# Down projection by products: when staged pieces are loaded and split, where S2 is computed, who evicts the first sums, and when the residual is added

## The chip, the cores and the metric

The kernel runs on one core of a Trainium2 chip. The metric is the device time of one execution in microseconds (us). The engines named below are TensorE (PE in the profile, with its weight loads as PEld), VectorE (DVE), ScalarE (ACT), GpSimd (POOL), and SyncE (SP), whose queue issues nearly all DMA transfers of this kernel.

## The reference, cut to what matters

The program is a two-layer decoder trunk over 1024 tokens of width 1024, in float32. Each layer has a mixer and a gated feed-forward part; the change concerns the last matrix product of the feed-forward part, in both layers.

```python
D_MODEL = 1024; SEQ = 1024; DEPTH = 2; D_FF = 2816

def conv_glu_ffn(x, w_up, conv_w, conv_b, w_down):
    h = causal_depthwise_conv(x @ w_up, conv_w, conv_b)
    gate, val = jnp.split(h, 2, axis=-1)
    return (jax.nn.silu(gate) * val) @ w_down      # (1024 x 2816) @ (2816 x 1024)

for layer in range(DEPTH):
    h = h + mixer(rmsnorm(h, ...))                 # even_mixer or odd_mixer
    h = h + conv_glu_ffn(rmsnorm(h, ffn_norm[layer]), ffn_up[layer], ffn_conv_w[layer],
                         ffn_conv_b[layer], ffn_down[layer])
return rmsnorm(h, final_norm)
```

## The kernel before, in words

**Precision.** Every float32 operand is *split*: ACT casts it to float32r (the high part, `h`), and DVE subtracts that from the source (the low part, `l`; "the low" in what follows). The function `split` does both. A product of two operands is three matmuls, hi·hi, hi·lo and lo·hi, each of a 128x128 weight block with a 128x512 block of tokens.

**The stage.** The 2816 hidden values are 22 blocks f of 128. Blocks 0 to 15 go through the down projection in two groups g of eight (`EIGHTS`), blocks 16 to 21 (`PLAIN`) directly and afterwards. Within a group the weights and the hidden values are cut into 2 x 2 blocks and multiplied with seven block products in place of eight (Strassen's scheme in Winograd's form). The hidden side's sums for that (`hids`, in DRAM) are made in the up projection that runs before. The weight side's sums are made in the stage: S1 = x21 + x22, S2 = S1 - x11, x11 - x21, and later S4 = x12 - S2.

**Quads and products.** Four output blocks form a quad: `Quad(g, oc, form)` with oc 0 or 4. A quad of form A makes the products "11", "2", "3" and "4" (with x11, S2, x11 - x21 and x22), a quad of form B makes "1", "21" and "22" (with S1, x12 and S4). Their order is, for each g: A oc 0, A oc 4, B oc 0, B oc 4. These are 28 products per layer (`steps_`), each of two half-products e of 12 matmuls, so 56 places t in one stage. The matmuls' tiles carry the quad's name: dq000A is layer 0, g 0, oc 0, form A; dq114B is layer 1, g 1, oc 4, form B. In instruction lists the product and e follow (dq000A111: product 11, e 1).

**Preparation of weights.** Two steps ahead of each product, `prep` runs the quad's step: load, sums and split of its weights (`x11`, `s2`, `s3`, `x22` for A, `s1`, `x12`, `s4` for B). S1 and S2 are stored to DRAM (`sums`) by the A quad and loaded again by the B quad. Whole weights come into two buffers (tag wst), half ones into four (`t2`), split weights wh and wl into three.

**Pieces.** The hidden side of a product comes in two *pieces* of 512 KB. `bring` loads one into a buffer br (a ring of four, tag t4, which the up projection also uses) and splits it at once into AH/AL (products 11, 2, 3, 4) or TH/TL (products 1, 21, 22). `stage` does the same with a plain block (hr), and `residual_in` loads 512 KB of the residual (hd) and adds it to hT, the sum that all products end in. The list `beside` holds such calls by group and form; one is taken behind each half-product as long as the list lasts.

**Evictions.** Four PSUM banks of 128x512 are used. After every half-product the bank's running sum goes to hT: by ACT as a copy where nothing stands in hT yet (group 0, oc 0, form A; L929), otherwise by DVE as an addition (L931). The residual lies in DRAM (hdr); half of it is loaded straight into hT for oc 4 at the start of the stage (L1058), the other half comes through `residual_in` in the second group.

**Order.** The code lists the work; a scheduler then orders each engine's instructions by its own estimates of times, and `tc.issue_after(x)` keeps what is issued under it behind x. Each engine, and each queue, then runs in order. The last block of the up projection (f = 21) has edits too: its Tail does the convolution's taps (L690), gate and store (`hid` and cv, L707) of the block before, while the first quad's weights and pieces come in.

## Time and profile before

| What | Value |
| --- | --- |
| Median of 3 runs | 2156.36 us (2156.1 to 2157.13) |
| Profiled execution | 2156.32 us, its span 2154.6 us |
| TensorE, busy | 2102.5 us, 98% of the span |
| DVE, busy | 1599.4 us, 74% |
| ACT, busy | 1062.9 us, 49% |
| Granted TensorE clock, mean | 0.996 |
| First to last product matmul, layer 0 | 781.91 to 947.19 us |
| First to last product matmul, layer 1 | 1907.00 to 2073.48 us |
| Loads of pieces (L808) | 56 of 512 KB, 5.5 us from issue to landing (median) |

Times in rows of the trace count from the start of the span. A row of a timeline reads: start, duration, engine (SPq is SyncE's queue), line, operation, what it writes and from what, shape, count, and in brackets the idle time of the engine just before with what ended it. Rows of a window read: stretch, its length, then the busy time and number of instructions of PE, PEld, DVE, ACT and POOL, the granted clock (1.00 is full speed), the share of the DMA engines that was busy, and GB/s. Rows of waits read: engine, its tile and line, what it waited for, total us, times, the longest.

### The profile page before, as it was taken

What the parts mean: (1) busy time and instruction counts of PE and PEld (TensorE: products, weight loads), DVE (VectorE), ACT (ScalarE), POOL (GpSimd) and SP (SyncE); (2) the same over time, 40 slices, a digit from 0 to 9 for tenths busy, and PEclk for the clock granted to TensorE, in tenths of its full rate; (3) what the DMA queues carried; (4) which work ended last, traced back from release to release, by engine and by line L of the source; (5) the groups of instructions that cost most, each with busy time, mean ns of one, the idle gap of its engine ahead of it and who ended that gap; (6) DMA issues with size and microseconds to landing.
All of it is one profiled execution on the core that took longest, in us unless ns stands there. A gap on an engine that the chain in (4) does not pass through costs nothing. (4 is left out here: it accounts for less than half of the span.)

```text
span 2154.6 us, 25867 instructions
## 1 busy us (share of the span) xinstructions
PE 2102.5 (98%) x9673; PEld 1720.3 (80%) x9673; DVE 1599.4 (74%) x2306; ACT 1062.9 (49%) x1485; POOL 74.7 (3%) x121
## 2 busy tenths in 40 slices
PE   8999999999999999999999999899999999999998
PEld 7888888788888877788778888788788888877787
DVE  6655647998888778855566666868998888778854
ACT  5333544655445554333556575744655554455323
POOL 0000001000000000000111111000000000000000
PEclk9999999999999999999999999999999999999999
DMA  4211342333232268641221211542333332268612
GB/s 145 59 49 44 108 147 92 103 103 118 94 117 94 77 208 301 229 126 64 74 65 47 83 50 55 166 148 88 98 123 98 98 117 93 98 229 281 222 49 79
DMA packets 265382, 249.98 MB, mean 116 GB/s; under 512 B 10384, under 2 KB 214992, under 8 KB 265256
## 3 DMA queue, kind: packets, MB, share of 16 engines
q1 hardware_dynamic: 264920, 247.83, 36.1%
q8 instruction: 76, 1.25, 0.2%
q0 software_dynamic: 192, 0.30, 0.1%
q14 instruction: 50, 0.41, 0.1%
q10 hardware_dynamic: 144, 0.20, 0.0%
HBM read 181.93 MB, written 64.26 MB: 114 GB/s over the span
## 5 line engine op out<-in xcount | busy, mean ns | idle before, releaser
L121 ACT CAST wh<-wst 128x1024 fp32r<-128x1024 f32 (+1 forms) x87 | 86.3, 992 | 224.6 <-PE op L368 45.1
L121 DVE TENSOR_TENSOR wl<-wst,wh 128x1024 fp32r<-128x1024 f32 (+1 forms) x87 | 100.1, 1151 | 98.4 <-ACT wh L121 98.2
L668 PE MATMUL X<-TH,wh 128*128 128x512 f32 x384 | 150.0, 391 | 1.8 <-ACT u L1012 1.4
L668 PE MATMUL X<-TH,wl 128*128 128x512 f32 x384 | 149.7, 390 | 0.7 <-DVE wl L362 0.7
L668 PE MATMUL X<-TL,wh 128*128 128x512 f32 x384 | 149.5, 389 | 0.0
L361 ACT CAST wh<-wst 128x1024 fp32r<-128x1024 f32 x96 | 100.2, 1050 | 74.2 <-PE YZ L668 49.6
L362 DVE TENSOR_TENSOR wl<-wst,wh 128x1024 fp32r<-128x1024 f32 x96 | 116.6, 1220 | 12.1 <-ACT wh L361 12.1
L690 DVE SCALAR_TENSOR_TENSOR cg<-g,par_c,cg 128x1023 f32<-128x1023 f32 x88 | 112.8, 1282 | 6.9 <-ACT cg L684 5.8
L690 DVE SCALAR_TENSOR_TENSOR cv<-v,par_c,cv 128x1023 f32<-128x1023 f32 (+1 forms) x88 | 112.5, 1278 | 0.1
L668 PE MATMUL YZ<-AH,wh 128*128 128x512 f32 x240 | 93.5, 389 | 0.0
L668 PE MATMUL YZ<-AL,wh 128*128 128x512 f32 x240 | 93.4, 389 | 0.0
L668 PE MATMUL YZ<-AH,wl 128*128 128x512 f32 x240 | 93.4, 389 | 0.0
L1012 ACT COPY u<-X 128x512 f32<-128x512 f32 x40 | 23.5, 587 | 138.0 <-PE X L668 138.0
L668 PEld LDWEIGHTS X<-TH,wh 128*128 128x128 f32 x384 | 72.1, 188 | 18.6 <-ACT u L1012 2.6
L668 PEld LDWEIGHTS X<-TH,wl 128*128 128x128 f32 x384 | 72.1, 188 | 16.6 <-DVE wl L362 1.6
L668 PEld LDWEIGHTS X<-TL,wh 128*128 128x128 f32 x384 | 72.1, 188 | 14.9
L1032 DVE TENSOR_TENSOR v<-p,u 128x512 f32<-128x512 f32 x40 | 27.7, 692 | 68.8 <-ACT u L1022 68.8
L368 PE MATMUL op<-AH,wh 128*128 128x512 f32 x192 | 76.3, 397 | 0.6 <-ACT hT_o L543 0.6
L368 PE MATMUL op<-AH,wl 128*128 128x512 f32 x192 | 74.9, 390 | 0.0
L368 PE MATMUL op<-AL,wh 128*128 128x512 f32 x192 | 74.8, 390 | 0.0
L684 ACT ACTIVATE cg<-g,par_c 128x1024 f32<-128x1024 f32 x44 | 54.8, 1246 | 28.8 <-DVE g L1034 24.2
L1557 ACT ACTIVATE P<-P,sm 128x128 f32<-128x128 f32 (+3 forms) x64 | 49.7, 777 | 29.9 <-DVE sm L1554 29.6
(815 smaller groups left out, 6305.2 us busy)
## 6 DMA issues: line engine op xcount, KB each, us to landing
wst<-in_ffn_up_dram SPq DMA_DIRECT2D x88, 512.0 KB, 3.8
br<-hids SPq DMA_DIRECT2D x56, 512.0 KB, 5.5
wst<-in_mix_w_in_dram SPq DMA_DIRECT2D x40, 512.0 KB, 3.7
wst<-in_mix_w_out_dram SPq DMA_DIRECT2D x32, 512.0 KB, 4.2
hids<-cv SPq DMA_DIRECT2D x32, 512.0 KB, 3.0
hdr<-hT_o SPq DMA_DIRECT2D x32, 256.0 KB, 2.0
hids<-t SPq DMA_DIRECT2D x32, 256.0 KB, 2.4
hid<-cv SPq DMA_DIRECT2D x12, 512.0 KB
```

The lines of the kernel that those rows point to most:

```text
L121: did = self.nc.scalar.copy(wh[:, :k, :m], w[:, :k, :m]), self.eng.tensor_tensor(wl[:, :k, :m], w[:, :k, :m], wh[:, :k, :m].bitcast(F32), ...
L361: return (act.copy(h, src), (eng or dve).tensor_tensor(l, src, h.bitcast(F32), op=ALU.subtract))
L362: (eng or dve).tensor_tensor(l, src, h.bitcast(F32), op=ALU.subtract))
L368: last_mm = pe.matmul(ps, a[:, k], b[:, k, s], start=(k == 0 and i == 0), stop=(k == DC - 1 and i == 2))
L668: last = pe.matmul(ps, a[:, k0 + k], b[:, k], start=(first and k == 0 and i == 0), stop=(k == 3 and i == 2), skip_group_check=True)
L684: act.activation(self.cg, self.g, AF.Identity, scale=taps[2](f), bias=bias(f))
L690: dve.scalar_tensor_tensor(dst[:, dl:], src[:, :T - dl], taps[j](c), dst[:, dl:], op0=ALU.mult, op1=ALU.add)
L1012: act.copy(u2, X)
L1032: dve.tensor_tensor(v[:, HALF[1]], p5, u3, op=ALU.add)
L1557: act.activation(Pt[:, :n], Pt[:, :n], AF.Exp, bias=low, scale=-1.0, accum_out=sm[:, 6:7])
```

## The change

The separate loads and splits: `bring`, `stage` and `residual_in` now issue the load at once and return a function that does the split (or the addition). A table by place t says where each split stands (`AT_FIRST` to `AT_PLAIN`); its load is issued `AHEAD` = 3 half-products earlier. A split is held behind the previous half-product's eviction and the last cast of weights. The first pieces come in the last block of the up projection.

S2 is written into the buffer of x11, split as one operand of 1024 columns, and stored by one transfer of 512 KB; x11 - x21 is therefore made in step `s2`, ahead of it. `sums` has another layout in DRAM. The first quad's x22 is loaded whole into the buffer that cv of block 20 leaves. Each later quad's first two weight loads are issued at two steps, no longer both at one.

All quads of form A in group 0 are evicted by ACT as copies. All eight parts of the residual are loaded and added at places in the second group. The store of the last hidden block (cv021 to `hid`) moves behind the first half-product.

```diff
@@ -41,2 +41,10 @@
+
+AHEAD = 3
+AT_FIRST = (2, 4)
+AT_B0 = (5, 7, 8, 10, 12, 14)
+AT_A1 = (15, 16, 18, 19, 21, 22, 24, 25)
+AT_B1 = (28, 30, 32, 34, 36, 38)
+AT_RES = (29, 33, 37, 41, 45, 47, 49, 51)
+AT_PLAIN = (43, 44, 46, 48, 50, 52)
 OPS = {"11": 0, "2": 1, "4": 2, "3": 3, "21": 4, "22": 5, "1": 6}
@@ -597,3 +605,3 @@
     hids = [[dram.tile([P, 7, 4, H], F32, name=f"hids{i}{g}") for g in EIGHTS] for i in range(2)]
-    sums = {(i, g, q): [dram.tile([P, 2, 4, P], F32, name=f"sum{i}{g}{q}{j}") for j in range(2)]
+    sums = {(i, g, q): [dram.tile([P, DC, P], F32, name=f"sum{i}{g}{q}{j}") for j in range(2)]
             for i in range(2) for g in EIGHTS for q in (0, 4)}
@@ -705,3 +713,5 @@
                 f, to, k = self.f, hids[ly][self.f // 8 % 2], self.f % 8 // 2
-                if f >= PLAIN[ly][0][0]:
+                if f == NF - 1:
+                    return
+                elif f >= PLAIN[ly][0][0]:
                     nc.sync.dma_start(hid[ly][:, f], self.cv)
...
@@ -794,3 +805,3 @@
             nc.sync.dma_start(r, hid[ly][:, f])
-            split(*slots[slot], r)
+            return lambda: split(*slots[slot], r)
...
@@ -845,3 +856,3 @@
                                                  name=f"{n}{self.name}")
-                    nc.sync.dma_start(t if n == "s1" else two(t), src)
+                    return nc.sync.dma_start(t if n == "s1" else two(t), src)
@@ -857,9 +868,15 @@
                     else:
-                        wst("x21", self.block(0, self.oc + 2, 2))
-                        small("x22", lambda e: self.block(1, self.oc + 2 + e, 1))
+                        last["sp"] = wst("x21", self.block(0, self.oc + 2, 2))
+                        if self.g == 0 and self.oc == 0:
+                            t = w2[1].tile([P, T], F32, tag="cv0", name=f"x22{self.name}")
+                            t = t.rearrange("p (k m) -> p k m", k=DC)
+                            nc.sync.dma_start(two(t), self.block(1, self.oc + 2, 2))
+                            self.raw["x22"] = [one(t, e) for e in range(2)]
+                        else:
+                            small("x22", lambda e: self.block(1, self.oc + 2 + e, 1))
                 elif i == 0:
-                    wst("s1", self.sum[0].rearrange("p e k m -> p (e k) m"))
+                    wst("s1", self.sum[0])
                 else:
                     wst("x12", self.block(1, self.oc, 2))
-                    small("s2", lambda e: self.sum[1][:, e])
+                    small("s2", lambda e: one(self.sum[1], e))
@@ -869,2 +886,5 @@
+            def whole(self, n, src):
+                last["cast"], last["low"] = split(*self.pair(n), src)
+
             def split2(self, n, src):
...
@@ -880,17 +900,16 @@
                 for e in range(2):
-                    dve.tensor_tensor(s[e], one(self.raw["x21"], e), self.raw["x22"][e],
-                                      op=ALU.add)
-                    nc.sync.dma_start(self.sum[0][:, e], s[e])
+                    last["sum"] = dve.tensor_tensor(s[e], one(self.raw["x21"], e),
+                                                    self.raw["x22"][e], op=ALU.add)
+                    nc.sync.dma_start(self.sum[0][:, 4 * e:4 * e + 4], s[e])
             def s2(self):
-                s = self.raw.pop("s")
+                t, a, s = self.raw["x21"], self.raw.pop("x11"), self.raw.pop("s")
+                dve.tensor_tensor(t, a, t, op=ALU.subtract)
                 for e in range(2):
-                    dve.tensor_tensor(s[e], s[e], one(self.raw["x11"], e), op=ALU.subtract)
-                    nc.sync.dma_start(self.sum[1][:, e], s[e])
-                self.split2("2", s)
+                    dve.tensor_tensor(one(a, e), s[e], one(a, e), op=ALU.subtract)
+                nc.sync.dma_start(self.sum[1], a)
+                self.whole("2", a)
             def s3(self):
-                t, a = self.raw.pop("x21"), self.raw.pop("x11")
-                dve.tensor_tensor(t, a, t, op=ALU.subtract)
-                split(*self.pair("3"), t)
+                self.whole("3", self.raw.pop("x21"))
...
@@ -927,6 +946,6 @@
                 at = st["hT"][:, self.oc + 2 * row + e, s]
-                if self.form == "A" and self.g == 0 and self.oc == 0:
-                    act.copy(at, ps)
+                if self.form == "A" and self.g == 0:
+                    did = act.copy(at, ps)
                 else:
-                    dve.tensor_tensor(at, ps, at, op=ALU.add)
+                    did = dve.tensor_tensor(at, ps, at, op=ALU.add)
                 if n in ("4", "21", "22"):
...
@@ -946,3 +966,3 @@
                 if q.form == "A":
-                    loads = {2: (0, 1)}.get(i, ())
+                    loads = {1: (0,), 2: (1,)}.get(i, ())
                 else:
@@ -993,2 +1013,3 @@
                 quads[0].load(0)
+                came = [b() for b in first_[:2]]
             w, nxt = ws.pop(f), f + 1 if f + 1 < NF else None
@@ -1011,3 +1032,8 @@
             u2 = t2(f"u2{ly}{f}")
-            act.copy(u2, X)
+            u2_ = act.copy(u2, X)
+            if not nxt:
+                with tc.issue_after(u2_.ins):
+                    for do in came:
+                        do()
+                came = [b() for b in first_[2:4]]
             prev.conv_v(0)
@@ -1027,5 +1053,2 @@
                 quads[0].load(1)
-                with tc.issue_after(u3_.ins):
-                    for b in first_[:2]:
-                        b()
             prev.sums()
@@ -1044,7 +1067,10 @@
             prev.ident()
-        for b in first_[2:4]:
-            b()
+        with tc.issue_after(u3_.ins), tc.issue_after(last["sum"].ins):
+            for do in came:
+                do()
         prep(1)
-        for b in first_[4:6]:
-            b()
+        came = [b() for b in first_[4:6]]
+        with tc.issue_after(last["cast"].ins), tc.issue_after(last["low"].ins):
+            for do in came:
+                do()
         prev.rest()
@@ -1056,4 +1082,2 @@
         hT = st["hT"]
-        for c in range(4, DC):
-            nc.sync.dma_start(hT[:, c], hdr[:, c])
@@ -1077,18 +1101,35 @@
             nc.sync.dma_start(r, hdr[:, c])
-            dve.tensor_tensor(hT[:, c], hT[:, c], r, op=ALU.add)
+            return lambda: (None, dve.tensor_tensor(hT[:, c], hT[:, c], r, op=ALU.add))
+
-        beside = {(0, "A"): first_[6:] + brings(0, ("1", "21", "22")),
-                  (0, "B"): brings(1, ("11", "2", "3", "4")),
-                  (1, "A"): [x for c, b in enumerate(brings(1, ("1", "21", "22")))
-                             for x in [b] + ([lambda c=c: residual_in(c)] if c < 4 else [])],
-                  (1, "B"): [lambda i=i: stage(PLAIN[ly][0][0] + i, i) for i in range(6)]}
+        pieces = {}
+        for at, ps in ((AT_FIRST, first_[6:]), (AT_B0, brings(0, ("1", "21", "22"))),
+                       (AT_A1, brings(1, ("11", "2", "3", "4"))),
+                       (AT_B1, brings(1, ("1", "21", "22"))),
+                       (AT_RES, [lambda c=c: residual_in(c) for c in range(DC)]),
+                       (AT_PLAIN, [lambda i=i: stage(PLAIN[ly][0][0] + i, i) for i in range(6)])):
+            for t, p_ in zip(at, ps):
+                pieces[t] = p_
+        came, prev_did = {}, None
         for n, (q, i) in enumerate(steps_):
-            todo = beside[q.g, q.form]
             for e in range(2):
-                q.prod(q.prods[i], e)
+                t = 2 * n + e
+                for t_ in range(t + 1 if t else 0, t + 1 + AHEAD):
+                    if t_ in pieces:
+                        came[t_] = pieces.pop(t_)()
+                did = q.prod(q.prods[i], e)
                 if e == 0 and n + 2 < len(steps_):
                     prep(n + 2)
-                if todo:
-                    todo.pop(0)()
+                if t == 0:
+                    with tc.issue_after(last["sp"].ins):
+                        nc.sync.dma_start(hid[ly][:, NF - 1], prev.cv)
+                    prev = None
+                if t in came:
+                    with ExitStack() as behind:
+                        behind.enter_context(tc.issue_after(last["cast"].ins))
+                        if prev_did is not None:
+                            behind.enter_context(tc.issue_after(prev_did.ins))
+                        came.pop(t)()
+                prev_did = did
             if n == len(steps_) - 2:
```

The first place is ACT's queue around the first quad of layer 0. AH and TH are the high parts of pieces br, wh those of weights; 0040 reads layer 0, group 0, product 4, piece 0; a bank keeps the name of product 11 for all four products; L929 and, after the change, L948 copy sums to hT. Before:

```order
L361 CAST wh68_5826<-x11004A_5743 128x1024
L361 CAST AH_83<-br0040_5751 128x2x512
L361 CAST AH_83<-br0041_5769 128x2x512
L929 COPY hT0_f0_5719<-dq000A110_5724 128x512
L929 COPY hT0_f0_5719<-dq000A111_5755 128x512
L361 CAST TH0_2559<-br0010_5792 128x1024
L929 COPY hT0_f0_5719<-dq000A110_5724 128x512
L929 COPY hT0_f0_5719<-dq000A111_5755 128x512
L361 CAST TH0_2559<-br0011_5809 128x1024
```

After:

```order
L948 COPY hT0_f0_5716<-dq000A110_5719 128x512
L369 CAST wh65_5686<-x11000A_5539 128x1024
L369 CAST AH_83<-br0030_5692 128x2x512
L369 CAST AH_83<-br0031_5694 128x2x512
L706 ACTIVATE cg021_5674<-cg021_5674 128x1024
L369 CAST wh66_5733<-x21000A_5633 128x1024
L948 COPY hT0_f0_5716<-dq000A111_5746 128x512
L948 COPY hT0_f0_5716<-dq000A110_5719 128x512
L369 CAST wh67_5775<-x22000A_5635 128x4x128 x2
L369 CAST AH_83<-br0040_5717 128x2x512
```

Before, the copies of the oc 0 quad come in pairs between the casts of pieces for products 4 and 1. After, the copy of half-product 0 of product 11 (dq000A110) stands first; two piece casts, the activation of the last up-projection block and a weight cast stand between it and the copy of half-product 1 (dq000A111).

The second place is SP's queue in the same stretch. Before:

```order
L808 DMA br0040_5751<-hids00_251 128x1024
L808 DMA br0041_5769<-hids00_251 128x1024
L707 DMA hid0_249<-cv021_5673 128x1024
L846 DMA x21004A_5745<-in_ffn_down_dram 128x4x256
L808 DMA br0010_5792<-hids00_251 128x1024
L1058 DMA hT1_f0_5715<-hdr_85 128x1024 x4
L808 DMA br0011_5809<-hids00_251 128x1024
L883 DMA sum0040_257<-s0004A_5830 128x512
```

After:

```order
L819 DMA br0031_5694<-hids00_251 128x1024
L910 DMA sum0001_256<-x11000A_5539 128x1024
L819 DMA br0040_5717<-hids00_251 128x1024
L857 DMA x11004A_5690<-in_ffn_down_dram 128x4x256
L819 DMA br0041_5744<-hids00_251 128x1024
L819 DMA br0010_5760<-hids00_251 128x1024
L857 DMA x21004A_5737<-in_ffn_down_dram 128x4x256
L819 DMA br0011_5796<-hids00_251 128x1024
L1126 DMA hid0_249<-cv021_5675 128x1024
L819 DMA br00210_5823<-hids00_251 128x1024
```

The residual loads into hT (L1058) are gone from between br0010 and br0011, S2 goes out in one store from x11's buffer (sum0001 from x11000A), and the store of cv021 stands behind br0011.

The third place is DVE's queue at the start of the second group's first quad (dq010A), where DVE evicts. TL is the low of a piece, wl that of a weight, hd a part of the residual. Before:

```order
L362 TENSOR_TENSOR wl80_6306<-x21010A_6188,wh80_6305 128x1024
L931 TENSOR_TENSOR hT0_f0_5719<-dq010A110_6290,hT0_f0_5719 128x512
L1078 TENSOR_TENSOR hT0_f0_5719<-hT0_f0_5719,hd00_6335 128x1024
L362 TENSOR_TENSOR TL0_2560<-br01211_6443,TH0_2559 128x1024
L931 TENSOR_TENSOR hT0_f0_5719<-dq010A111_6321,hT0_f0_5719 128x512
L362 TENSOR_TENSOR wl81_6352<-x220010A_6190,wh81_6351 128x4x128
L362 TENSOR_TENSOR wl81_6352<-x221010A_6191,wh81_6351 128x4x128
L881 TENSOR_TENSOR s0014A_6394<-x21014A_6311,x220014A_6313 128x512
L931 TENSOR_TENSOR hT0_f0_5719<-dq010A110_6290,hT0_f0_5719 128x512
L881 TENSOR_TENSOR s1014A_6395<-x21014A_6311,x221014A_6314 128x512
```

After:

```order
L370 TENSOR_TENSOR wl79_6264<-x11010A_6098,wh79_6263 128x1024
L950 TENSOR_TENSOR hT1_f0_5712<-dq004B11_6186,hT1_f0_5712 128x512
L370 TENSOR_TENSOR wl80_6299<-x21010A_6178,wh80_6298 128x1024
L370 TENSOR_TENSOR TL0_2560<-br0110_6226,TH0_2559 128x1024
L950 TENSOR_TENSOR hT0_f0_5716<-dq010A110_6284,hT0_f0_5716 128x512
L1102 TENSOR_TENSOR hT0_f0_5716<-hT0_f0_5716,hd00_6244 128x1024
L950 TENSOR_TENSOR hT0_f0_5716<-dq010A111_6312,hT0_f0_5716 128x512
L370 TENSOR_TENSOR wl81_6343<-x220010A_6180,wh81_6342 128x4x128
L370 TENSOR_TENSOR wl81_6343<-x221010A_6181,wh81_6342 128x4x128
L901 TENSOR_TENSOR s0014A_6382<-x21014A_6302,x220014A_6304 128x512
L370 TENSOR_TENSOR TL0_2560<-br0111_6269,TH0_2559 128x1024
L950 TENSOR_TENSOR hT0_f0_5716<-dq010A110_6284,hT0_f0_5716 128x512
```

Before, up to two weight lows, sums and a piece's low stand between the evictions of dq010A. After, S2's low and x11 - x21's low (wl79, wl80) and one piece (br0110) stand ahead of its first eviction, and the residual's addition comes between the first and the second.

11 lines of the change are left out of this document (6 added, 5 removed).

## The prediction

> **What bounds the kernel now.** I read the busy table first, then TensorE's waits, and then windows over the two stages that the change edits. TensorE is the bound: whatever is won or lost has to appear as TensorE waiting less or more.
>
> ```profile
> span 2154.6 us, 25867 instructions
> PE 2102.5 (98%) x9673; PEld 1720.3 (80%) x9673; DVE 1599.4 (74%) x2306; ACT 1062.9 (49%) x1485; POOL 74.7 (3%) x121
> ```
>
> The products of the down projection stand on L922 (tiles dq...). The windows of that line alone (columns: stretch, its length, PE busy with its number of matmuls, PEld busy, granted clock, DMA share, GB/s) are both stages, one undisturbed quad, and the two A quads of the second group in each layer:
>
> ```profile
> 781.91:947.19 165.28, 156.56 (x672) 126.09 (x671) 0.99 0.70 235
> 1907.00:2073.48 166.48, 158.04 (x672) 127.19 (x671) 0.98 0.68 228
> 851.87:868.19 16.32, 16.32 (x74) 13.51 (x72) 1.00 0.79 270
> 868.19:914.55 46.36, 44.57 (x194) 35.72 (x192) 1.00 0.67 222
> 1994.43:2040.84 46.41, 44.61 (x194) 35.72 (x192) 1.00 0.69 227
> ```
>
> The quad at 851.87 is 72 matmuls (the window touches two more) without idle time: 16.32 / 72 = 0.2267 us from start to start. A half-product (12) therefore takes 2.72 us, an A quad (96) 21.76, and a stage's 672 matmuls 152.3. The stages take 165.28 and 166.48, so **12.96 + 14.16 = 27.1 us** are lost in them. That is the ceiling of this change. Two A quads need 43.52; the second group takes 46.36 and 46.41, so 2.84 + 2.89 = 5.7 of the loss lie there, and 21.4 in the first group. Who TensorE waited for, in layer 0:
>
> ```profile
> PE dq004A L922 <- ACT wh L361: 3.6, 2, 3.2
> PE dq000A L922 <- DVE wl L362: 1.7, 2, 0.9
> PE dq010A L922 <- DVE hT_f L931: 1.4, 2, 1.2
> PE dq000A L922 <- ACT hT_f L929: 0.9, 1, 0.9
> ```
>
> Neither ACT nor DVE is short of time: they stand behind pieces that have not landed. In the same stretch ACT was idle 14.7 and 22.4 us for pieces (br), each a 512 KB load:
>
> ```profile
> L361 ACT CAST AH<-br 128x1024 fp32r<-128x1024 f32 x14 | 14.6, 1052 | 14.8 <-DMA br<-hids 14.7
> L361 ACT CAST TH<-br 128x1024 fp32r<-128x1024 f32 x12 | 12.6, 1050 | 24.5 <-DMA br<-hids 22.4 <-PE dq004B L922 2.1
> br<-hids SPq DMA_DIRECT2D x56, 512.0 KB, 5.5
> ```
>
> The largest wait, step by step: SP issues four residual loads and then a piece. The piece lands 9.2 us later, ACT's cast of it is released at 814.02, DVE's half of the split follows, and only behind that stand DVE's sum for S2, ACT's cast of it, and the matmul.
>
> ```profile
> 803.01 1.74 SPq L1058 DMA_DIRECT2D hT_f<-hdr  x4
> 804.85 1.29 SPq L808 DMA_DIRECT2D br<-hids  x1
> 814.02 1.05 ACT L361 CAST TH<-br 128x1024 fp32r<-128x1024 f32 x1 [3.52 <-DMA br<-hids]
> 815.10 1.22 DVE L362 TENSOR_TENSOR TL<-br,TH 128x1024 fp32r<-128x1024 f32 x1
> 816.25 0.69 DVE L888 TENSOR_TENSOR s0004A<-s0004A,x11004A 128x512 f32<-128x512 f32 x1
> 816.97 0.62 ACT L361 CAST wh<-s0004A 128x512 fp32r<-128x512 f32 x1 [1.89 <-DVE s0004A L888]
> 817.64 0.80 PE L922 MATMUL dq004A<-AH,wh 128*128 128x512 f32 x1 [3.22 <-ACT wh L361]
> ```
>
> **The change, part by part.** *Late residual and copies by ACT.* The 2 MB of residual loads at 803.01 leave the stretch; eight 512 KB loads now lie in the second group. Eight evictions of dq004A go from DVE to ACT, and four more residual adds come to DVE, per layer:
>
> ```profile
> L929 ACT COPY hT_f<-dq000A x8: 574/587/590, 787.2 to 809.9; 128x512 f32<-128x512 f32 x8
> L931 DVE TENSOR_TENSOR hT_f<-dq004A,hT_f x8: 684/688/692, 812.2 to 839.3; 128x512 f32<-128x512 f32 x8
> L1078 DVE TENSOR_TENSOR hT_f<-hT_f,hd x8: 1216/1222/1227, 871.8 to 2019.4; 128x1024 f32<-128x1024 f32 x8
> ```
>
> DVE: -8 x 0.688 + 4 x 1.222 = -0.6 us; ACT: +8 x 0.587 = +4.7. Both are free while TensorE is fed; the cover is the 43.5 us of the two A quads.
>
> *S2 in A11's place.* Per A quad two casts (0.62) and two lows (about 0.68) become one of each over 1024 columns (1.05 and 1.22), and x21 = x11 - x21 is only moved ahead: about -0.3 us. Two stores become one; S2's later loads become runs of 512 bytes, as those of x22 already are. I take nothing: these loads are used three products later.
>
> *The first A quad, walked.* I keep the clock of the profiled execution, where TensorE starts this quad at 781.9 in both versions, and take starts from these rows; a pair of lows takes 2.36 us, hence 1.15 from one to the next, and 0.6 for a half-width one.
>
> ```profile
> 770.43 0.32 SPq L707 DMA_DIRECT2D hid<-cv  x1
> 776.67 0.59 ACT L1022 COPY u<-X 128x512 f32<-128x512 f32 x1 [2.13 <-PE X L668]
> 778.23 2.36 DVE L362 TENSOR_TENSOR AL<-br,AH 128x1024 fp32r<-128x1024 f32 x2 [0.26 <-ACT AH L361]
> wst<-in_ffn_down_dram SPq DMA_DIRECT2D x3, 512.0 KB, 3.5
> hids<-cv SPq DMA_DIRECT2D x32, 512.0 KB, 3.0
> ```
>
> Now x22 is loaded whole into the buffer of cv, so SP must wait for that store: 770.4 + 3.0 = 773.4, landed at 776.9. Behind it in SP's queue stands one piece, which needs a low of 774.1 anyway. DVE, in its new order: x21 + x22 (776.9), v behind u3 (777.3), the other half (777.9), the low of br0020 (778.5), g (779.7), the low of br0021 (780.3), x21 (781.4), a tap (782.5), S2's halves (783.7 and 784.3, done 785.0), a tap (784.9). ACT casts S2 from 785.4 to 786.4, DVE lowers it from 786.5 to 787.7. TensorE's products 11 end at 787.35 and its third matmul of product 2 needs that low at 787.8: **no stall, against 0.80 and 0.89 us before**. Next ACT casts br0030, br0031, runs the silu and casts x21 before it copies the second bank of product 11; at 0.95 us each that copy ends near 790.7. TensorE wants it at 790.07: **0.65 us, and 0.1 of slow restart**. Product 4 needs the low of br0041 at 800.5; my walk has it at 800.35, so I charge another 0.5 for this and for S2's low together, with 0 and 1.5 as bounds. The second A quad (from about 804.5) finds x11, x21 and S2 ready five products ahead. First group: 2 x 1.25 = 2.5 left of 21.4.
>
> *The second group.* There DVE evicts, and one late piece blocks it:
>
> ```profile
> 874.60 1.05 ACT L361 CAST TH<-br 128x1024 fp32r<-128x1024 f32 x1 [5.34 <-DMA br<-hids]
> 875.69 1.22 DVE L362 TENSOR_TENSOR TL<-br,TH 128x1024 fp32r<-128x1024 f32 x1 [2.63 <-ACT TH L361]
> 876.83 0.68 DVE L931 TENSOR_TENSOR hT_f<-dq010A,hT_f 128x512 f32<-128x512 f32 x1
> 877.66 0.47 PE L922 MATMUL dq010A<-AH,wh 128*128 128x512 f32 x1 [1.16 <-DVE hT_f L931]
> 868.19:891.95 23.76, 22.38 (x97) 17.68 (x96) 20.39 (x26) 7.35 (x9) 0.00 (x0) 1.00 0.71 229
> ```
>
> The ring of four buffers lets a piece be issued four places before its split, 10.9 us, where 5.5 are needed, so these waits go. But DVE (20.39 busy in the last row) stays nearly full in 21.76; I leave 0.5 per layer (bounds 0 and 2.84). Left over in all: 2.5 + 1.0 = 3.5, so the change saves 27.1 - 3.5 = **23.6 us**. The profiled execution took 2156.32, 1.7 over its span and 0.04 under the median: 2132.7, said as **2133**.
>
> *One rule against the rows.* After the long wait the clock is halved, and in layer 1 too, where only 1.58 and 0.29 us of waiting precede:
>
> ```profile
> 817.30:820.70 3.40, 3.06 (x7) 2.44 (x8) 3.06 (x5) 3.40 (x5) 0.00 (x0) 0.51 0.95 269
> 1923.20:1926.60 3.40, 3.32 (x7) 2.28 (x8) 3.40 (x5) 1.36 (x3) 0.00 (x0) 0.51 0.86 334
> 1922.26 0.50 PE L922 MATMUL dq100A<-AH,wh 128*128 128x512 f32 x1 [1.58 <-ACT hT_f L929]
> ```
>
> A halved stretch gives 1.00 - 0.51 of 3.4, or 1.7 us, away. By these rows even two short waits close together could keep one per layer: 2136. The Trainium skill (TensorE: Matmul & The Clock Gate, Part 1) has the clock fall only after a whole idle window of about 3.4 us; by it the waits left over would never do this, and the sum stays. The row of 1923.20 disagrees with it.
>
> **The rivals.** (1) *The new wait bites.* x22's load waits for a store, and DVE's sum waits for x22 ahead of v, g and two pieces in its queue. For it: that queue is in order. Against: the DMA engines are idle then. If x22 lands 9.2 us after its issue, like the piece at 804.85, instead of 3.5, the chain moves by 5.7 us, TensorE waits 5.2 longer and runs 1.7 at half speed: 2 x 6.9 = 13.8 back, 2147.
>
> (2) *The first quad stays short of DMA.* Sixteen transfers of 0.52 MB stand between 778 and 805 in the new queue, 311 GB/s, and the stages' first groups ran at about that rate already. For it: a share of 0.95 at 269 GB/s above. Against: the residual's 2 MB are gone. If the first quads keep their waits, which are half of the first group's 21.4, and only the rest goes: 27.1 - 10.7 - 3.5 = 12.9 saved, 2143.
>
> (3) *Slower: the fixed places.* Each split is tied behind the eviction before it, and so stands ahead of the next one. From the last place of the first group's A quads on, where DVE evicts, there are 28 such places per layer. A weight's low, a piece's low and an eviction are 1.22 + 1.22 + 0.69 = 3.13 us against 2.72, or 0.41 over; with a sum (0.69) 1.1 over. If nothing carries to the lighter places and half of them have the sum, that is 56 places in both layers at 0.75 on average, 42 us: 2156 - 24 + 42 = 2174. It decides from 23.6 / 56 = 0.42 us per place. Against it: an eviction has a whole half-product of slack, since two banks alternate, and 20.39 us of DVE work fit 21.76.
>
> **How the numbers follow.** Forecast 0.62, own range 2129.5 to 2139 (nothing left over; the upper bounds 3.0 + 5.7 plus a clock loss per layer, less what cannot all come at once). Rival 1 0.16, rival 2 0.12, rival 3 0.07, and 0.03 for gains and losses that cancel. A measurement of this kernel tells about 0.2% (4.3 us) from no change: faster 0.62 + 0.16 + 0.12 = 0.90, same 0.03, slower 0.07. The range goes from 2129.5, nearly the ceiling of 27.1, to rival 1's 2147.
>
> **What would show it.** Right: both stages near 154 us; no wait of dq004A for ACT's cast; waits of dq000A for ACT's copy under 1 us; ACT's idle time for pieces down; no halved clock inside the stages. Wrong: x21 + x22 starting after 778 with DVE idle before it; dq010A waiting longer for evictions; a product waiting for a piece; the up projection's last block losing time, since its queues take the first pieces earlier. If TensorE runs through and the time still does not fall, the loss was never these waits.

## The result, and the profile after

The changed kernel takes **2138.32 us** (median of 4 runs, 2136.61 to 2143.3) where the kernel before takes 2156.23 beside it; the ratio is 0.9924, with a 95% interval of 0.9904 to 0.9944. It is 17.9 us faster. The forecast was 2133 (range 2129.5 to 2147): sign and range hold, the gain is three quarters of the 23.6 us that were forecast.

The first lines of the page after:

```profile
span 2136.6 us, 25861 instructions
PE 2097.7 (98%) x9673; PEld 1721.0 (81%) x9673; DVE 1599.6 (75%) x2290; ACT 1068.9 (50%) x1493; POOL 74.7 (3%) x121
```

The two windows over the product line (now L941), columns as in the prediction:

```profile
780.05:936.82 156.77, 153.77 (x672) 125.56 (x671) 1.00 0.72 237
1897.77:2055.31 157.54, 153.59 (x672) 125.59 (x671) 1.00 0.71 233
```

The stages took 165.28 and 166.48 us and take 156.77 and 157.54: 8.51 + 8.94 = 17.45 us of the 18.0 by which the span fell. Ahead of the first stage 1.86 us are gained, of which 1.3 are already there at 260 us, in code that did not change; between the stages 1.14 us are lost, and 0.17 behind them. TensorE's waits in the up projection ahead of the first stage are the same as before, within 0.1 us each. Against 152.34 us for 672 matmuls the stages now lose **4.43 + 5.20 = 9.6 us, where 27.1 were lost and 3.5 were forecast**. No clock below 1.00 is left in either.

The waits of TensorE in the two stages, in the form shown before:

```profile
PE dq014A L941 <- DVE hT_f L950: 1.1, 1, 1.1
PE dq000A L941 <- ACT hT_f L948: 0.8, 1, 0.8
PE dq000A L941 <- DVE wl L370: 0.5, 1, 0.5
PE dq000A L941 <- DVE AL L370: 0.4, 1, 0.4
...
PE dq114A L941 <- DVE hT_f L950: 1.4, 1, 1.4
PE dq100A L941 <- DVE AL L370: 1.1, 1, 1.1
PE dq100A L941 <- ACT hT_f L948: 0.9, 1, 0.9
PE dq100A L941 <- DVE wl L370: 0.5, 1, 0.5
```

dq004A's wait of 3.2 us for S2's cast is gone, and so is its twin in layer 1, which read before:

```profile
PE dq104A L922 <- ACT wh L361: 3.5, 2, 3.2
```

ACT's waits for pieces are gone too. In layer 0's stage it stood idle for 14.7 and 22.4 us for them; now the same rows (busy us and mean ns, then the idle time ahead) read:

```profile
L369 ACT CAST AH<-br 128x1024 fp32r<-128x1024 f32 x12 | 12.4, 1050 | 0.2 <-DMA br<-hids 0.2
L369 ACT CAST TH<-br 128x1024 fp32r<-128x1024 f32 x12 | 12.6, 1051 | 0.0
```

Four waits of TensorE are left per layer, the same four. A wait's row shows less than what it costs: counted from start to start of matmuls, with the late start and the slower first matmul after it, the four (S2's low, the copy, the low of br0041, the eviction in the second group) cost 1.21, 1.04, 0.69 and 1.36 us in layer 0 and 0.88, 1.22, 1.32 and 1.66 in layer 1. All other quads run at 21.76 and 16.32 us, without loss.

**S2's low.** SP issues x22 behind the store it waited for; DVE stands idle for it; then its queue runs without a gap to S2's low, and TensorE waits for that; 0.4 of the 1.21 us are already lost to S2's cast, just ahead of the low. From the timeline of layer 0:

```profile
771.84 0.38 SPq L873 DMA_DIRECT2D x22000A<-in_ffn_down_dram  x1
776.23 0.69 DVE L901 TENSOR_TENSOR s0000A<-x21000A,x22000A 128x512 f32<-128x512 f32 x1 [2.94 <-DMA x22000A<-in_ffn_down_dram]
785.78 1.23 DVE L370 TENSOR_TENSOR wl<-x11000A,wh 128x1024 fp32r<-128x1024 f32 x1
787.05 0.50 PE L941 MATMUL dq000A<-AH,wl 128*128 128x512 f32 x1 [0.52 <-DVE wl L370]
```

**The copy and br0041.** The copy of product 11's second bank stands behind a silu and a weight cast, as forecast. The low of br0041 stands behind two sums, which wait for x21 of the next quad:

```profile
787.87 1.06 ACT L706 ACTIVATE cg<-cg 128x1024 f32<-128x1024 f32 x1
788.83 1.03 ACT L369 CAST wh<-x21000A 128x1024 fp32r<-128x1024 f32 x1
789.76 1.07 ACT L948 COPY hT_f<-dq000A 128x512 f32<-128x512 f32 x2
...
798.39 0.69 DVE L901 TENSOR_TENSOR s0004A<-x21004A,x220004A 128x512 f32<-128x512 f32 x1 [0.99 <-DMA x21004A<-in_ffn_down_dram]
799.61 1.22 DVE L370 TENSOR_TENSOR AL<-br,AH 128x1024 fp32r<-128x1024 f32 x1
800.88 0.50 PE L941 MATMUL dq000A<-AL,wh 128*128 128x512 f32 x1 [0.42 <-DVE AL L370]
```

**The second group.** There DVE stands idle for x12, with an eviction behind it in its queue. From the timeline:

```profile
890.62 0.69 DVE L928 TENSOR_TENSOR s20010B<-x12010B,s20010B 128x512 f32<-128x512 f32 x1 [2.06 <-DMA x12010B<-in_ffn_down_dram]
891.23 1.22 DVE L370 TENSOR_TENSOR TL<-br,TH 128x1024 fp32r<-128x1024 f32 x1
892.37 0.68 DVE L950 TENSOR_TENSOR hT_f<-dq014A,hT_f 128x512 f32<-128x512 f32 x1
893.20 0.47 PE L941 MATMUL dq014A<-AH,wh 128*128 128x512 f32 x1 [1.13 <-DVE hT_f L950]
```

The window of that quad, with DVE busy in 17.38 of 23.20 us:

```profile
881.00:904.20 23.20, 22.07 (x98) 17.96 (x97) 17.38 (x21) 7.15 (x9) 0.00 (x0) 1.00 0.71 244
```

### The profile page after: what moved, and what is told of

Same layout as the page of the kernel before. It is cut to its first block, busy times and chain, and to the rows that moved or that the text cites. A ratio compares the mean times of both kernels' runs of the same rounds, so it can differ in the third digit from the quotient of the medians.

```text
span 2136.6 us, 25861 instructions
## 1 busy us (share of the span) xinstructions
PE 2097.7 (98%) x9673; PEld 1721.0 (81%) x9673; DVE 1599.6 (75%) x2290; ACT 1068.9 (50%) x1493; POOL 74.7 (3%) x121
## 3 DMA queue, kind: packets, MB, share of 16 engines
q8 instruction: 76, 1.25, 0.2%
## 5 line engine op out<-in xcount | busy, mean ns | idle before, releaser
L1033 ACT COPY u<-X 128x512 f32<-128x512 f32 x40 | 23.6, 589 | 136.3 <-PE X L676 136.3
```

The lines of the kernel that those rows point to most:

```text
L1033: u2_ = act.copy(u2, X)
```

## The experiments

All are edits of the changed kernel, and each has one profile. "Loss" is what the two stages take beyond 152.34 us each, from the profile of that run, layer 0 + layer 1; the ratio is to the kernel before in the same batch. How far two profiles of one order differ is seen in e1: up to 2 us in a stage, 0.8 in the sum. Differences under about 2 us in the summed loss are therefore not read.

| Run | Loss, us | Median, us | Ratio (95%) |
| --- | --- | --- | --- |
| before | 12.94 + 14.14 = 27.1 | 2156.23 | |
| changed kernel | 4.43 + 5.20 = 9.6 | 2138.32 | 0.9924 (0.9904 to 0.9944) |
| e1 load at the split | 6.40 + 4.04 = 10.4 | 2140.77 | 0.9919 (0.9899 to 0.9938) |
| e2 places packed | 5.20 + 3.00 = 8.2 | 2140.31 | 0.9912 (0.9896 to 0.9928) |
| e3 residual early | 4.32 + 6.10 = 10.4 | 2142.47 | 0.9925 (0.9908 to 0.9943) |
| e4 S2 in its own tiles | 6.17 + 4.74 = 10.9 | 2144.35 | 0.9930 (0.9915 to 0.9945) |
| e5 splits not held | 3.70 + 4.37 = 8.1 | 2139.91 | 0.9911 (0.9890 to 0.9931) |
| e6 packed, residual early | 4.32 + 3.61 = 7.9 | 2140.86 | 0.9913 (0.9894 to 0.9933) |
| e7 as e6, not held | 7.73 + 6.21 = 13.9 | 2145.35 | 0.9937 (0.9913 to 0.9961) |
| e8 first pieces late | 9.55 + 5.06 = 14.6 | 2147.86 | 0.9948 (0.9931 to 0.9964) |
| e9 x22 early | 6.21 + 5.03 = 11.2 | 2138.51 | 0.9913 (0.9899 to 0.9928) |
| e10 five parts undone | 15.98 + 18.88 = 34.9 | 2168.64 | 1.0054 (1.0038 to 1.0071) |
| e11 order mended | 2.30 + 1.73 = 4.0 | 2134.66 | 0.9894 (0.9879 to 0.9908) |
| e12 S4 held | 3.84 + 3.25 = 7.1 | 2138.46 | 0.9909 (0.9890 to 0.9928) |

### What made the gain: parts undone alone

```diff
 # e1
-AHEAD = 3
+AHEAD = 0
-                for t_ in range(t + 1 if t else 0, t + 1 + AHEAD):
+                for t_ in range(t, t + 1):
```

> The load of each piece of the stage is written right ahead of its own split, no longer three half-products earlier (AHEAD 3 to 0); the fixed places stay. The stages of the changed kernel take 156.77 and 157.54 us from their first product to the next stage's first matmul, of which 4.43 and 5.20 are lost. Theory A: the distance in the code is what brings the pieces in time. A piece takes 5.5 us to land, a half-product 2.72, so each split then waits some 5 us in an ordered queue and the stages lose at least 5 us more each. Theory B: when a load leaves is decided by when one of the four buffers comes free, that is by the places of the splits; the two stages then stay within 0.5 us of 156.77 and 157.54, and the run also shows how far two profiles of one order of instructions differ.

The loss is 10.4 us against 9.6. With the load written beside its split, the instructions of all engines and of SP's queue stand in exactly the same order as with three half-products ahead. The number in the code does nothing here. That is theory B; that a load's place is set by when one of the four buffers comes free is argued from it, no run changed the number of buffers. The run is thus also a repeat, and its two second groups (24.64 and 22.43 us for dq014A and dq114A, 23.15 and 23.44 in the changed kernel) show how much the wait for x12 varies.

```diff
 # e2
-AT_FIRST = (2, 4)
-AT_B0 = (5, 7, 8, 10, 12, 14)
-AT_A1 = (15, 16, 18, 19, 21, 22, 24, 25)
+AT_FIRST = (0, 1)
+AT_B0 = (2, 3, 4, 5, 6, 7)
+AT_A1 = (16, 17, 18, 19, 20, 21, 22, 23)
...
```

> The fixed places are packed as the kernel before had its pieces: one per half-product from the start of each pair of quads, places 0 to 7, 16 to 23, 28 to 41 (pieces and residual parts in turn) and 44 to 49. All else is as in the changed kernel. Theory A: the spread of the places is a main part of the gain. With the pieces packed, 4 MB of pieces and the weights of two quads are wanted within the first 22 us, splits wait for pieces in ACT's and DVE's queues, and evictions and weights stand behind them: the first group loses 8 us or more per layer, up to the 10 of the kernel before. Theory B: what cost time before were the residual's 2 MB and the scheduler's own placing; with those gone packed places cost under 2 us per stage.

The loss is 8.2: the spread of the places alone is not what gained. Theory A misses by far (8 us or more per layer were expected). In layer 0 the scheduler interleaves the two A quads again, and together they lose 5.2 us; in layer 1 3.0; the second group loses nothing.

```diff
 # e3
-                if self.form == "A" and self.g == 0:
+                if self.form == "A" and self.g == 0 and self.oc == 0:
...
+        for c in range(4, DC):
+            nc.sync.dma_start(hT[:, c], hdr[:, c])
...
-                       (AT_RES, [lambda c=c: residual_in(c) for c in range(DC)]),
+                       (AT_RES, [lambda c=c: residual_in(c) for c in range(4)]),
```

> One part is undone: half of the residual (2 MB) is again loaded straight into hT ahead of the first quads, DVE again adds the sums of dq004A, and four residual parts are added in the second group instead of eight. Theory A: these 2 MB were what made the pieces late. At the rate of the first group (about 300 GB/s) they take some 7 us of all DMA engines; dq000A and dq004A together take 5 to 9 us longer per layer than the 46.6 and 47.1 of the changed kernel. Theory B: with the pieces at spread places there is slack for 7 us of transfers, and the two quads stay within 1 us.

dq000A and dq004A take 46.90 us in layer 0 and 47.24 in layer 1, against 46.58 and 47.06. Theory B: the 2 MB alone do no harm that can be told from noise. That the pieces around them have slack is the reading that fits.

```diff
 # e4
-                t, a, s = self.raw["x21"], self.raw.pop("x11"), self.raw.pop("s")
-                dve.tensor_tensor(t, a, t, op=ALU.subtract)
+                a, s = self.raw["x11"], self.raw.pop("s")
                 for e in range(2):
-                    dve.tensor_tensor(one(a, e), s[e], one(a, e), op=ALU.subtract)
-                nc.sync.dma_start(self.sum[1], a)
-                self.whole("2", a)
+                    dve.tensor_tensor(s[e], s[e], one(a, e), op=ALU.subtract)
+                    nc.sync.dma_start(one(self.sum[1], e), s[e])
+                self.split2("2", s)
...
```

> One part is undone: S2 is computed in its own two tiles of 512 columns, cast and lowered in two halves and stored in two transfers, and x11 - x21 is made one step later again. Theory A: this part carries no time of its own, about 0.3 us of ACT and DVE per quad; S2's first half may even be ready earlier for TensorE. dq000A stays within 1 us of 24.82 and 25.30, everything else within 0.3. Theory B: the order mattered (S2's low late behind other work, x21's buffer held a step longer, so x11 and x21 of the next quads come later): dq000A or dq004A loses 2 us or more per layer.

dq000A takes 27.57 us against 24.82, dq100A 25.66 against 25.30: outside theory A's bound in layer 0, inside in layer 1. The median is 6 us above the changed kernel's, but the stages differ by only 1.3 in all. The kernel before also took 2.2 us longer in this batch than beside the changed kernel. What S2's place is worth alone stays between nothing and 3 us.

```diff
 # e5
-                    with ExitStack() as behind:
-                        behind.enter_context(tc.issue_after(last["cast"].ins))
-                        if prev_did is not None:
-                            behind.enter_context(tc.issue_after(prev_did.ins))
-                        came.pop(t)()
+                    came.pop(t)()
```

> The splits keep their places in the code, but are no longer held behind the previous half-product's eviction and the last cast of weights; the scheduler places them by its estimates, as before the change, and puts several pieces' lows ahead of where they stood. Theory A: holding them is what made the gain, since no eviction and no weight then stands behind a piece that has not landed; without it the stages lose 3 to 10 us more each than the 4.4 and 5.2 of the changed kernel. Theory B: the pieces land early enough in either order, and the two stages together stay within 2 us of 314.3. Third (the fixed places cost time): the stages get shorter by 2 us or more.

The loss is 8.1 us, 1.6 less than with the splits held, within what e1 leaves open. Theory B; holding the splits by itself neither gained nor cost anything that these profiles can tell.

### Parts undone together

e6 joins the edits of e2 and e3, e7 those of e2, e3 and e5.

> Two parts are undone at once that each changed the stages by under 2 us alone: packed places and the early residual (2 MB ahead of the first quads, DVE adds the sums of dq004A). The splits are still held. Theory A: each was covered by the slack that the other leaves; together the loads of the first 25 us exceed what the DMA engines moved there (about 350 GB/s) by 2 MB, 6 us, and the first group loses 8 to 12 us per layer, as before the change. Theory B: the gain comes from elsewhere (splits held, first pieces in the up projection, S2 in place), and the first group loses no more than the 5 and 3 us it lost with packed places alone.

> As e6, and the splits are not held either: what is left of the change is S2 in x11's place, the first pieces earlier in the last block of the up projection, x22 whole, and the next quad's weights loaded at two steps. Theory A: places, residual and holding together are the gain; the two stages come back to a loss of 25 us in all or near it (27.1 before). Theory B: the parts that are left are what matters; the loss stays under 15 us.

e6 loses 7.9 us, so even packed places and the early residual together bring nothing back, as theory B of e6 had it (layer 1 loses 0.6 more than with packed places alone). Without the holds the same kernel loses 13.9. So holding is worth 6.0 us there, and nothing where the places are spread (e5). e7 stays under 15, its theory B: 13.2 of the 17.5 us come from what is still left of the change, or from several of its parts at once.

```diff
 # e8
-                came = [b() for b in first_[:2]]
...
-            if not nxt:
-                with tc.issue_after(u2_.ins):
-                    for do in came:
-                        do()
-                came = [b() for b in first_[2:4]]
...
+                with tc.issue_after(u3_.ins):
+                    for b in first_[:2]:
+                        b()()
...
-        with tc.issue_after(u3_.ins), tc.issue_after(last["sum"].ins):
-            for do in came:
-                do()
+        for b in first_[2:4]:
+            b()()
         prep(1)
-        came = [b() for b in first_[4:6]]
-        with tc.issue_after(last["cast"].ins), tc.issue_after(last["low"].ins):
-            for do in came:
-                do()
+        for b in first_[4:6]:
+            b()()
```

> One part is undone: the first six pieces are loaded and split in the last block of the up projection as before the change (the first two behind u3, the others without a hold). Theory A: this part gained only in the first quad: dq000A and dq100A get 1 to 4 us longer, since pieces for product 2 and 3 land and are split later, and the rest stays within 1 us. Theory B: it is where the gain of the whole first group lies: dq000A and dq004A together lose 8 us or more per layer. Third: the first pieces stand in the way of S2's low; without them the quad gets shorter by up to 1 us.

This is the one part that costs clearly alone, and it does so in layer 0: 14.6 us lost, 5.0 more. dq000A takes 29.76 us (24.82), dq100A 25.98 (25.30); the quads behind lose nothing more. That is theory A in kind, but its 1 to 4 us are passed in layer 0 and not reached in layer 1. A piece's low now stands between the two halves of S2 on DVE, and S2's cast comes late; the last row shows TensorE's wait for it:

```profile
787.05 0.68 DVE L909 TENSOR_TENSOR x11000A<-s0000A,x11000A 128x512 f32<-128x512 f32 x1
788.38 1.23 DVE L370 TENSOR_TENSOR AL<-br,AH 128x1024 fp32r<-128x1024 f32 x1 [0.65 <-ACT AH L369]
789.52 0.69 DVE L909 TENSOR_TENSOR x11000A<-s1000A,x11000A 128x512 f32<-128x512 f32 x1
...
791.34 0.50 PE L941 MATMUL dq000A<-AH,wh 128*128 128x512 f32 x1 [2.69 <-ACT wh L369]
```

Layer 1 has this wait as well (2.5 us), but fewer of the others. In layer 0 two waits for ACT's copies follow, of 0.70 and 1.74 us, and behind the second TensorE's matmuls start 0.43 us apart, no longer 0.227: from 800.62 to 804.37, eight of them take 3.75 us in place of 1.81. The granted clock there stands third from the end of the window:

```profile
800.62 0.66 PE L941 MATMUL dq000A<-AH,wh 128*128 128x512 f32 x1 [1.74 <-ACT hT_f L948]
800.20:803.60 3.40, 2.98 (x7) 2.36 (x8) 3.40 (x5) 2.47 (x3) 0.00 (x0) 0.59 0.90 279
```

e10 joins the edits of e2, e3, e4, e5 and e8.

> Five parts are undone together: spread places, late residual with ACT's copies for oc 4, held splits, first pieces earlier, S2 in x11's place. Left of the change are x22 loaded whole, and the next quad's weights loaded at two steps. Each part alone changed the two stages' loss (9.6 us) by -1.4 to +5; residual, places and holding together brought it to 13.9. Theory A: the parts cover for one another, and together they are the gain: the loss comes back to 22 to 29 us (27.1 before), with dq004A waiting for S2's cast again. Theory B: the weights loaded at two steps are what keeps dq004A fed; the loss stays below 19 us and dq004A has no wait over 1.5 us for a cast of weights.

The loss is 34.9 us and the kernel is slower than the one before. Theory A, and above its bound. The excess over 27.1 lies mainly in the same wait, now 5.4 us in layer 0 and 10.3 in layer 1, where it was 3.2 and 3.2; why it is longer than before was not taken apart. Alone, the five parts gave -1.4, +0.8, +1.3, -1.6 and +5.0 us, 4.1 in all; together they give +25.2. The old chain is back, here in layer 1. The wait first:

```profile
PE dq104A L942 <- ACT wh L369: 10.3, 1, 10.3
```

And the timeline of SP, ACT and DVE ahead of it:

```profile
1934.74 1.74 SPq L1079 DMA_DIRECT2D hT_f<-hdr  x4
1936.58 1.25 SPq L819 DMA_DIRECT2D br<-hids  x2
...
1945.59 1.04 ACT L369 CAST TH<-br 128x1024 fp32r<-128x1024 f32 x1 [7.25 <-DMA br<-hids]
...
1946.67 1.23 DVE L370 TENSOR_TENSOR TL<-br,TH 128x1024 fp32r<-128x1024 f32 x1 [5.38 <-ACT TH L369]
1947.81 0.69 DVE L908 TENSOR_TENSOR s0104A<-s0104A,x11104A 128x512 f32<-128x512 f32 x1
...
1948.53 0.62 ACT L369 CAST wh<-s0104A 128x512 fp32r<-128x512 f32 x1 [0.54 <-DVE s0104A L908]
```

The residual goes ahead of two pieces, a piece lands late, its low stands ahead of S2's subtraction, and S2's cast ahead of the matmul: step by step the chain that the prediction read in the kernel before. From 1936 to 1949 us the DMA engines are busy for 0.97 of the time, at 359 GB/s: the piece is late in a stretch where they have no room left (in the first 25 us of the changed kernel's stage 0.90, at 312 GB/s). None of the five parts alone brings the chain back, nor do three of them (in e7 the second A quads wait 0.5 us at most). Which two, three or four are enough was not tried further.

### What is left: the four waits

```diff
 # e9
-                self.cg, self.cv = (w2[1].tile([P, T], F32, tag=t, name=f"{t[:2]}{ly}{f}")
-                                    for t in ("cg", f"cv{f % 2}"))
+                self.cg, self.cv = (w2[1].tile([P, T], F32, tag=t, name=f"{n}{ly}{f}")
+                                    for n, t in (("cg", "cg" if f < NF - 1 else "cv0"),
+                                                 ("cv", f"cv{f % 2}")))
...
-                self.conv_v(1)
+                with tc.issue_after(last["low"].ins) if self.f == NF - 1 else nullcontext():
+                    self.conv_v(1)
...
-                            t = w2[1].tile([P, T], F32, tag="cv0", name=f"x22{self.name}")
+                            t = w2[1].tile([P, T], F32, tag="cg", name=f"x22{self.name}")
```

> One load is freed: the first quad's x22 goes into the buffer of cg of block 20, which is free once it has been read (768.5 us in layer 0 of the changed kernel), no longer into that of cv, which first has to be stored (SP waited from 768.9 to 771.8 for it); cg of block 21 takes cv's buffer instead. The order of instructions on every engine is otherwise that of the changed kernel. Theory A: x22's landing sets S2: DVE stood idle for 2.94 us ahead of x21 + x22, its queue behind it ran without a gap to S2's low, and TensorE waited for that low (0.31 + 0.10 + 0.69 + 0.11 us late in layer 0). x22 lands some 3 us earlier, the low 1 us or more earlier, and the 1.0 to 1.2 us at product 2's third matmul are gone in both layers; the copy of product 11's second half, behind on ACT, may still cost its 1.0. Theory B: DVE's queue is bound by something else behind it (the piece cast by ACT at 777.5, g from TensorE); the wait stays within 0.3 us.

The hold on `conv_v(1)` keeps the order of instructions: SP, ACT and DVE have the same one as in the changed kernel. Theory A. SP issues x22 at once behind the store, and TensorE's wait for S2's low is gone in both layers:

```profile
769.88 0.32 SPq L718 DMA_DIRECT2D hid<-cv  x1
770.25 0.43 SPq L875 DMA_DIRECT2D x22000A<-in_ffn_down_dram  x1
775.92 0.69 DVE L903 TENSOR_TENSOR s0000A<-x21000A,x22000A 128x512 f32<-128x512 f32 x1 [1.31 <-DMA x22000A<-in_ffn_down_dram]
```

It took 5.67 us to land beside the store's own transfer (4.39 behind it), so of 2.9 us of earlier issue, counted from TensorE's start of the stage, 1.6 remained. That was enough. dq000A takes 24.04 us (24.82), dq100A 24.45 (25.30); the copy still costs 1.06 and 1.39. The whole loss did not fall, since dq014A's wait for x12 was long in this run (it lost 3.95 us).

```diff
 # e12
+                with (tc.issue_after(last["did"].ins) if (self.g, self.oc) == (1, 0)
+                      else nullcontext()):
                     for e in range(2):
                         dve.tensor_tensor(t[e], one(a, e), t[e], op=ALU.subtract)
```

> One thing is held: in the second group's first B quad, S4 = x12 - S2 stands behind an eviction of the half-product ahead of its step, so that DVE no longer waits for x12 ahead of the evictions of dq014A and dq114A. Nothing in the first group changes. Theory A: what those quads lose (1.39 and 1.68 us in the changed kernel; 0.7 to 3.9 in the runs that keep its order there) is DVE standing idle for x12 (2.06 and 2.35 us) in front of an eviction; with S4 held both quads take 21.76 us, within 0.3. Theory B: DVE is simply full there, as the prediction had it; the same work is done in the same stretch and the quads still lose 1 us or more.

dq014A and dq114A take 21.76 us each, without any loss: theory A. In the time itself this can't be told from the changed kernel (ratio 0.9909 and 0.9924). The eviction now follows the piece's low directly, and S4 comes some 14 us later (counted from the start of the stage), in time:

```profile
891.13 1.23 DVE L370 TENSOR_TENSOR TL<-br,TH 128x1024 fp32r<-128x1024 f32 x1
892.27 0.68 DVE L952 TENSOR_TENSOR hT_f<-dq014A,hT_f 128x512 f32<-128x512 f32 x1
...
906.10 0.68 DVE L930 TENSOR_TENSOR s20010B<-x12010B,s20010B 128x512 f32<-128x512 f32 x1
```

e11 joins e9 and e12 with three more edits of order (e9's hold on `conv_v(1)` is replaced by the one on `prev.rest()`):

```diff
 # e11, beside e9 and e12
-            for do in came:
-                do()
+            came[0]()
+        prep(2)
+        with tc.issue_after(last["low"].ins):
-        prev.rest()
+            prev.rest()
...
-        came, prev_did = {}, None
+        came, prev_did = {1: came[1]}, None
...
+                if t == AT_FIRST[1]:
+                    with tc.issue_after(last["cast"].ins), tc.issue_after(prev_did.ins):
+                        _, last["piece"] = came.pop(t)()
...
+                  with (tc.issue_after(last["piece"].ins) if (self.g, self.oc) == (0, 4)
+                        else nullcontext()):
                     last["sum"] = dve.tensor_tensor(s[e], one(self.raw["x21"], e),
```

> The changed kernel with the order mended at each place where TensorE still waits: x22 as in e9; the split of x11 - x21 is issued ahead of the last up-projection block's taps, and these are held behind its low; the split of br0031 comes one half-product later, so that ACT's copy of product 11's second half goes ahead of it; br0041 is split ahead of the next quad's S1, which is held behind its low; S4 of the second group's first B quad is held behind an eviction. Theory A: each remaining wait is a matter of one late weight or piece in front of needed work in an ordered queue, so that the order alone cures it: the first quads lose under 0.7 us (3.06 and 3.54 in the changed kernel), dq014A and dq114A under 0.3 (1.39 and 1.68), the two stages 2 us or less in all, and the time falls by 6 to 8 us from the changed kernel's 2138.3, to about 2131. Theory B: DVE is full in the first 14 us of the stage and the waits only move: the stages keep 6 us or more of loss and the time stays within 4 us of 2138.

The stages lose 4.0 us in all, 5.6 less than the changed kernel, and the time is **2134.66 us** (2134.14 to 2135.47), ratio 0.9894 (0.9879 to 0.9908): the fastest kernel here. It is theory A in kind, not in full size: 2 us or less and about 2131 were expected, and the time alone would also fit theory B (within 4 us of 2138). The waits for S2, for a piece's low and for x12 are gone. What is left in layer 0 are waits for ACT's copies:

```profile
PE dq000A L946 <- ACT hT_f L953: 0.8, 2, 0.6
PE dq004A L946 <- ACT hT_f L953: 0.6, 1, 0.6
```

ACT's timeline ahead of the first of them:

```profile
785.02 1.05 ACT L369 CAST AH<-br 128x1024 fp32r<-128x1024 f32 x1 [0.46 <-DMA br<-hids]
785.98 1.04 ACT L369 CAST wh<-x21000A 128x1024 fp32r<-128x1024 f32 x1
786.93 0.57 ACT L953 COPY hT_f<-dq000A 128x512 f32<-128x512 f32 x1
```

With x21's cast moved forward, it and br0030's stand ahead of the copy of product 11's first bank: that wait did move, as theory B had feared for all of them. In layer 1 one wait for a copy (0.8 us) and one of dq110A for an eviction (0.4) are left.

## Why the prediction was right or wrong

- **The ceiling** (27.1 us, in these two stages alone) was right: 17.45 of the 18.0 us of the span came from there, 0.55 net from the rest. What fell short is the share of it that was won: 9.6 us were left over where 3.5 were forecast, 6.6 for 2.5 in the first group and 3.1 for 1.0 in the second. So the sign "both stages near 154 us" was missed, by 2.8 and 3.5 us.
- **"Ready ahead: the second A quad"** was right: dq004A and dq104A take 21.76 us, no clock was halved, and the forecast lost nothing there.
- **"S2: no stall" failed**, by the term "landed at 776.9". I gave x22 the 3.5 us of the row of weight loads; it took 4.39, and it was issued 0.3 us later than my walk had it. On the prediction's clock (this run starts the stage 1.85 us earlier) it landed at 778.1, after the 778 that I had named as the sign of a wrong step, with DVE idle for 2.94 us. S2's cast and low cost 1.21 and 0.88 us, with the restarts. That is the mechanism of rival 1, at a small fraction of its price. Its "against", idle DMA engines, did not hold: they were busy for 0.71 of the time while x22 came, with a piece issued just behind it. e9 showed the cause.
- **The copy** (0.65 and 0.1 for the restart) was right in mechanism, and a little short: 1.04 and 1.22.
- **Product 4** was charged 0.5, bounds 0 and 1.5, together with S2's low. It took 0.69 and 1.32 alone; behind it stands x21 of the next quad, 6.8 us from issue (791.63) to the sum that used it (798.39), which my walk did not name. With three terms the first quads lost 3.06 and 3.54 us, against 1.25 each.
- **The second group** was charged 0.5 per layer because "DVE stays nearly full". It lost 1.39 and 1.68 for another reason: DVE was idle for 2.06 us, waiting for x12 in front of an eviction. e12 took that wait away and nothing was lost. S4's two subtractions, 1.4 us of DVE, moved behind the quad with it; but with 17.38 us busy of 23.20 DVE was not full even with them. The upper bound of 2.84 held here, but not in e9's layer 0 (3.95).
- **Rival 2** (short of DMA) falls: the piece waits are gone, although the DMA engines were busier over the stages (0.72 and 0.71, against 0.70 and 0.68).
- **Rival 3** (the fixed places) falls: the time fell, and e5 gains no more than noise without the holds.
- **One reason behind the forecast was not needed.** The prediction took the late residual as what frees the first quads, and the lead of the loads as what frees the second group. With the residual early again the long waits stay away (e3). With the new constant at 0 the order is the same (e1), so the lead was there without it, as the ring of four buffers in the prediction would have it; no run took the lead itself away. The gain is made by several parts that cover for one another (e10).
- **The clock.** The row that spoke for a halving after short waits did not apply: the waits left over, up to 1.42 us in a row, halved nothing. In e8 it did: 0.70 and 1.74 us of waiting, with some 0.7 us of work between, were enough. The other side, that only a long idle window halves it, does not hold either; see e9's row below.

## What to carry to other kernels

Where engines run ordered queues, look for the operation that waits for a load ahead of work that TensorE needs: three of the four waits left here were of that kind, each with DVE idle for 1 to 3 us in front of a load (2.94, 0.99 and 2.06), and each went or shrank when the operation was moved behind the needed one or its buffer came free earlier. For a load on such a path take the time of a load beside the traffic of that moment (4.4 to 6.8 us here from issue to use), not the median of a calmer row (3.5). And undo parts in groups, too: five parts that cost 4 us in all when undone one by one cost 25 us together.

## What was not expected of the hardware

The clock was halved after a single wait of 2.17 us in e9, and not after one of 2.31 us in e7. e9's matmul behind the wait:

```profile
894.77 0.76 PE L943 MATMUL dq014A<-AH,wh 128*128 128x512 f32 x1 [2.17 <-DVE hT_f L952]
```

The window of 3.4 us from there on, with the granted clock third from the end:

```profile
894.80:898.20 3.40, 3.40 (x9) 2.67 (x10) 2.16 (x3) 0.00 (x0) 0.00 (x0) 0.53 0.61 183
```

A matmul of e7 behind a longer wait, and the window from there on:

```profile
1993.32 0.50 PE L941 MATMUL dq110A<-AH,wh 128*128 128x512 f32 x1 [2.31 <-DVE hT_f L950]
```

```profile
1993.30:1996.70 3.40, 3.38 (x15) 2.81 (x16) 3.37 (x6) 0.24 (x1) 0.00 (x0) 1.00 0.59 177
```

So the length of the wait alone does not decide it. The Trainium skill (TensorE: Matmul & The Clock Gate, Part 1) puts the lower clock behind at least one idle window of about 3.4 us. e9's row disagrees, with 2.17 us of waiting. What does decide was not tried. The same load also varied from run to run with the same order of instructions: DVE waited 2.06 us for x12 in layer 0 of the changed kernel, and 3.55 us in e1.
